# Half of the low parts of the weights in the key-head stage, on GpSimd instead of VectorE

## The chip, the cores and the metric

The kernel runs on one core of a Trainium2 chip. The metric is the device time of one execution in microseconds, as the median of several runs; before the change it was 2585.1 us. The engines go by the names of the profile: PE is TensorE, DVE is VectorE, ACT is ScalarE, POOL is GpSimd, and SP issues most of the transfers. Each engine works through its own list of instructions in order and waits at an instruction until what it needs is there.

## What is computed

The reference is a two-layer trunk over 256 latent tokens and 256 context tokens of 2048 features, all in float32. Layer 1 is attention. Layer 2, which the text calls the delta layer, is a bidirectional gated DeltaNet; it projects the normalized tokens, runs a short convolution and solves a small triangular system in each chunk of 64 tokens:

```python
qkv, z, b_raw, a_raw = split_cols(h, DN_SPLITS)          # h @ w_in: 16 key heads, 32 value heads of 128
qkv = jax.nn.silu(depthwise_conv(qkv, conv_w))
...
kb = kf * bf[..., None]
lmat = jnp.where(strict, jnp.einsum('bhncd,bhnsd->bhncs', kb, kf) * decay, 0.0)
rhs = jnp.concatenate([vf * bf[..., None], kb * jnp.exp(gf)[..., None]], axis=-1)
sol = lax.linalg.triangular_solve(lmat + jnp.eye(CHUNK, dtype=F32), rhs, left_side=True, lower=True)
```

A scan over the chunks, a norm, a gate and an output projection follow.

## The kernel before

**Matrix products in two parts.** Activations and weights are each split into a high part in a rounded float32 form (float32r) and a low part, the remainder. A product is three matmuls for every block of 128 contraction rows: high x high, high weight x low activation, low weight x high activation. These are lines 90, 91 and 92 in `dense`; the tiles are `whi`, `wlo` for the weights and `hh`, `hl` for the activations. All three follow one another on PE for each block, so the low part of a weight tile is needed at almost the same moment as the high part.

**A unit of the projection.** `dunit` makes 128 outputs of the delta layer's input projection. `load_split` loads the unit's 128 x 2048 weights in two tiles of 128 x 1024 (`load_raw`, SP's queue, line 71; four `raw` buffers in rotation), and `split` makes of each tile the high part on ACT (line 77) and the low part on DVE (line 78): raw minus high, three buffers each for `whi` and `wlo`. A `raw` buffer is free again when its low part is made. 16 blocks of contraction, and so 48 matmuls, follow on PE. `dunit` is called for 67 units: one for strengths and decays (`U_BA`), 16 for the keys over all 512 tokens, 16 for the queries and 32 for the gates over 256 tokens, and two for the values of head 0. Later value units do not pass through it: in the scans, `hi` and `lo` do the same splitting at lines 1080 and 1088 from a list `W`, in an order of PE, DVE and ACT that is written out by hand.

**The key-head stage.** From about 1120 to 1764 us the kernel goes through the 16 key heads. `head` (a generator, cut into steps by `yield`) projects keys and queries, convolves them (`conv_taps`, line 561, DVE), transposes the keys (line 679, PE), makes the decays (line 711 on POOL, the product at line 713 on PE, the exponential at line 716 on ACT) and the systems of two directions (lines 731 to 737, DVE). `inverse` inverts the 32 x 32 blocks of two heads at a time: transposes into `L` (line 755, DVE), 31 steps of an outer product (line 768) and a subtraction (line 770) on DVE, a scaling on POOL (line 772), transposes (lines 775, 776, DVE), then products of blocks on PE (lines 786 and 798). `zunits` projects the gates. These three are woven by hand: six steps of `heads`, then for each further step of `heads` seven steps of `inverse`, with the gates' units dealt out between them.

POOL has little else in this stage: memsets (lines 751, 752, 762, 763), the two small operations on the key norms (lines 701 and 702), line 711 and line 772.

**What sets the order.** Outside the scans, the order of each engine's instructions is made by the framework's planner when the kernel is built, from the program's order and its own estimate of each instruction's time. It also inserts the semaphores. A change of the engine of one instruction can so change the order of others.

Of the kernel before, what the change touches and what calls it, by code (L numbers as in the profile page):

```python
# [26 lines left out]
def trunk_kernel(ctx: ExitStack, tc: tile.TileContext, g):  # L27
# [40 lines left out]
    # ---------------------------------------------------------------- helpers  # L68
# [5 lines left out]
    def split(raw, m=1024):  # L74
        hi = wp.tile([128, 1024], F32R, name="whi", tag="whi", bufs=3)
        lo = wp.tile([128, 1024], F32R, name="wlo", tag="wlo", bufs=3)
        A.copy(hi[:, :m], raw[:, :m])  # L77
        V.tensor_tensor(lo[:, :m], raw[:, :m], hi[:, :m].bitcast(F32), op=ALU.subtract)  # L78
        return hi, lo

    def load_split(src, n=2048):
        return [split(load_raw(src[:, c:min(n, c + 1024)], min(1024, n - c)), min(1024, n - c))
                for c in range(0, n, 1024)]
# [11 lines left out]
    def sliced(wsrc, units, k0, n, xh, xl, pst, first, last):  # L95
        # n contraction tiles of two units
        m = 128 * n
        raw = wp.tile([128, 1024], F32, name="raw", tag="raw", bufs=4)
        for e in range(2):
            nc.sync.dma_start(raw[:, m * e:m * e + m], wsrc[units[e]][:, 128 * k0:128 * k0 + m])  # L100
        w = split(raw, 2 * m)
        for e in range(2):
            dense(pst[e], [w], m * e, n, xh, xl, k0=k0, first=first, last=last)
# [3 lines left out]
    def adaln(l, ps, pm, tp, order, bufs=3, after=None):  # L107
        # a step for every two weight tiles
        wm, bmod, gain = ((g["ab_wm"], ab_bmod, ab_gain), (g["dn_wm"], dn_bmod, dn_gain))[l]
        for f0, n in order:  # L110
            # n blocks of 128 outputs from f0 on
# [35 lines left out]
    def adaln_lanes(l, ps, pm, tp, chunks, after=None):  # L147
        # the sums over the contraction tiles on the vector engine, those over the partitions at the end
# [36 lines left out]
    def rstd_bcast(squares, nb, dim, ps, tag, tp, sq_tag="sq"):  # L185
        # squares: for every block of tokens the tiles that add up to its squares, summed over the feature tiles
        ss = ps.tile([128, 4], F32, name="ss", tag=tag, bufs=1)
        for tb in range(nb):
            for i, t in enumerate(squares[tb]):
                PE.matmul(ss[:, tb:tb + 1], t, ones[:, 0:1], start=i == 0, stop=i == len(squares[tb]) - 1)  # L190
        ms = tp.tile([128, 4], F32, name="ms", tag="ms")
        V.tensor_scalar(ms[:, :nb], ss[:, :nb], 1.0 / dim, EPS, op0=ALU.mult, op1=ALU.add)  # L192
        rs = tp.tile([128, 4], F32, name="rs", tag="rs")
        P.tensor_tensor(rs[:, :nb], ms[:, :nb], half[:, :nb], op=ALU.pow)  # L194
        dg = tp.tile([128, 4, 128], F32, name="dg", tag=sq_tag)
        rb = ps.tile([128, 512], F32, name="rb", tag=tag, bufs=1)
        for tb in range(nb):
            V.tensor_scalar(dg[:, tb], ident, rs[:, tb:tb + 1], None, op0=ALU.mult)
            PE.matmul(rb[:, tb * 128:(tb + 1) * 128], ones, dg[:, tb], start=True, stop=True)
        return rb  # L200
# [4 lines left out]
    def add_squares(acc, srcs, first, tp, n=T, sq_tag="sq", last=False):  # L205
        # the last squares stay apart
# [29 lines left out]
    # ================================================================ layer 0  # L236
# [6 lines left out]
    with tc.tile_pool(name="s0", bufs=2) as tp, tc.tile_pool(name="s0p", bufs=1, space=PSUM) as ps:  # L243
# [6 lines left out]
        # squares, four feature tiles at a time  # L250
# [51 lines left out]
    with tc.tile_pool(name="ab", bufs=2, reuse_waits="tile") as tp, \  # L302
# [29 lines left out]
        def parts(src, name, n=T, scale=1.0, pool=None, bufs=1):  # L332
            # float32 as the sum of two float32r
# [16 lines left out]
        def attend(qT, kT, vT, h, bias=None, rope=None):  # L350
            # v to token-major
# [58 lines left out]
        # latent ranks and the shared rope key  # L410
# [98 lines left out]
    # ================================================================ layer 1  # L509
    # Tokens of a sequence go in two tiles of two chunks, (0, 3) and (1, 2); inside a tile the order is  # L510
    # (half of the chunk, chunk of the pair, token), so that a 32-partition quadrant is 2 * half + chunk,
    # while the keys are worked on, and (chunk of the pair, token) in the scans.
# [23 lines left out]
    def dunit(u, sl):  # L536
        w = load_split(DW[u])
# [29 lines left out]
    def tile_act(dst, src, func, halves):  # L567
        # to tile order, as (half, chunk, token) or (chunk, token)
# [9 lines left out]
    def by_pair(dst, src):  # L578
        # columns from (half, chunk, token) to (chunk, half, token)
        A.copy(dst.rearrange("p s (h b i) -> p s b h i", h=2, b=2), src.rearrange("p s (b h i) -> p s b h i", b=2, h=2))  # L580

    def by_chunk(dst, src):
        # rows from (half, chunk, token) to (chunk, token)
# [22 lines left out]
    def project(u, p):  # L606
        # output unit to the residual, back from tile order
# [5 lines left out]
    # the scans take over the room of the keys' tiles tag by tag, so that they begin as it is left  # L613
    with tc.tile_pool(name="dn", bufs=2, reuse_waits="tile") as tp, \
            tc.tile_pool(name="dnps", bufs=2, space=PSUM, reuse_waits="tile") as ps:
        # write strength and decay of all heads
# [3 lines left out]
        # of the keys: squared norms inverted, and norms, as the rows lie here and in the scans; of the queries, what  # L620
        # stands for the norm's epsilon once they are not normalized
# [35 lines left out]
        for d in range(2):  # L657
# [3 lines left out]
            # scan arrangement a: chunk h of a pair runs in direction (a + h) % 2  # L661
# [10 lines left out]
        def head(kh):  # L672
# [31 lines left out]
            # the decays [row, column]: forwards for the transposed system, backwards for the system  # L704
            # itself and, within the sequence, transposed
# [27 lines left out]
            for d in range(2):  # L733
                # of a 32-block only what lies on its side of the diagonal is read
# [8 lines left out]
        def inverse(sg):  # L743
            # (norm^2 / beta + L)^-1 of two heads, their keys not normalized, L the system forwards and its transpose backwards: of the
            # 32-blocks on the vector engine, with the unit on the partition
            NTu = NTs[sg].rearrange("p a k s h i -> p (a k s h) i")
            # as the blocks come and transposed
# [31 lines left out]
            # the block between the two halves of a chunk  # L779
# [42 lines left out]
        def mix(main, filler, n):  # L822
            # one step of the filler after every n of the main work
# [8 lines left out]
        def woven():  # L832
            # the heads one after the other, each with its products begun while the one before it ends
# [71 lines left out]
        def cut(t, i, shape):  # L905
            # piece i of a tile, in a shape
# [11 lines left out]
        # block-diagonal operands: the zeros stay, the blocks come from memory  # L918
# [14 lines left out]
        # of keys and values, the parts that the state's products take  # L933
# [6 lines left out]
        def blocks(dst, src):  # L940
            # [128, 2 (direction), 4, 64] in memory to [128, 2 (arrangement), 4, 128]
# [25 lines left out]
        def step(o, n):  # L967
            # one chunk in both directions, in four parts
# [68 lines left out]
        def finish(o):  # L1037
            # norm and gate of a head, in four parts
# [26 lines left out]
        # of the output products, units below NE take the heads below 12 early  # L1065
        NE = 8
        # weight tiles in the order of their use
# [23 lines left out]
        def tile_mm(p, j, k0, xh, xl, sl, first, last):  # L1091
            # the eight contraction tiles of weight tile j, one at a time
# [12 lines left out]
        def value_unit(q):  # L1105
            # q: unit number after those of head 0; its first step is 2 * q - 2
# [57 lines left out]
        for st in range(-2, 64 + LAG):  # L1164
# [27 lines left out]
            # what follows the products of the unit before  # L1192
# [77 lines left out]
def _layout(inputs):  # L1270
# [5 lines left out]
    def fm(a):  # [tok, feat] -> [128, feat/128, tok]  # L1276
        return np.ascontiguousarray(a.T.reshape(-1, 128, a.shape[0]).transpose(1, 0, 2))

    def units(w, kt=None):  # [K, C] -> [C/128, 128, K/128 * 128]
# [3 lines left out]
    def vec(v):  # [F] -> [128, F/128]  # L1283
# [25 lines left out]
    # neighbourhood bias, padded outside the window  # L1309
# [10 lines left out]
    # constants of the shapes alone  # L1320
# [10 lines left out]
    # gated delta layer  # L1331
# [45 lines left out]
```

## Time and profile before

| | |
|---|---|
| median of 3 runs | 2585.1 us (2583.42 to 2586.82) |
| span of the profiled execution | 2580.0 us |
| PE busy in it | 2499.2 us (97%) |
| DVE busy | 1852.2 us (72%) |
| ACT busy | 1146.6 us (44%) |
| POOL busy | 267.4 us (10%) |
| the key-head stage | about 1120 to 1764 us |

The span is the time from the first to the last instruction of one execution. Rows of groups read: line, engine, operation, output tile <- input tiles, shapes, count | busy us, mean ns of one | idle us of the engine just before them and what ended it. Rows of waits read: who waited <- for whom: us in total, times, the longest. A timeline row is start, length, engine, line, operation, and in brackets how long the engine had been idle and what ended that. Busy figures of PE are higher than its true use, as consecutive matmuls overlap in the record.

### The profile page before, as it was taken

The numbers are of one execution on the slowest core, as the hardware profiler recorded it, in microseconds if no ns is written. First come the engines' busy times: TensorE is split into PE (matmuls) and PEld (weight loads), VectorE is DVE, ScalarE is ACT, GpSimd is POOL, SyncE is SP. The second block draws the span as 40 slices with busy tenths as digits, with TensorE's granted clock in tenths as the row PEclk, the third lists the DMA queues.
The fourth block names the chain that finished last, engine by engine and source line by source line (L and its number), as shares of the span: only waits on it lengthen the run. The fifth ranks groups of instructions, "written<-read, shape, count | busy, mean of one in ns | idle before, by whom it ended". The sixth has DMA issues, their size and how long they took to land.

```text
span 2580.0 us, 43446 instructions
## 1 busy us (share of the span) xinstructions
PE 2499.2 (97%) x16586; PEld 2039.0 (79%) x16586; DVE 1852.2 (72%) x3543; ACT 1146.6 (44%) x2484; POOL 267.4 (10%) x261
## 2 busy tenths in 40 slices
PE   6999999999999999989999999999999999999998
PEld 4657888888767788768888889897777777777898
DVE  4544788773455687758999999987677777777754
ACT  4223323232333422377656655643444445445353
POOL 0000000000000000133212222310000000003000
PEclk9999999999999999999999999999999999999999
DMA  8872655532343376644454544563333433335454
GB/s 258 289 247 90 201 172 167 175 114 96 117 153 100 120 230 221 212 139 157 142 156 152 160 138 150 159 213 100 88 99 115 119 99 106 113 91 174 153 188 140
DMA packets 201810, 394.30 MB, mean 153 GB/s; under 512 B 68225, under 2 KB 109697, under 8 KB 201473
## 3 DMA queue, kind: packets, MB, share of 16 engines
q1 hardware_dynamic: 200448, 389.98, 47.9%
q8 instruction: 131, 2.15, 0.4%
q10 hardware_dynamic: 1152, 1.54, 0.2%
q14 instruction: 79, 0.64, 0.1%
HBM read 356.28 MB, written 35.13 MB: 152 GB/s over the span
## 4 chain that ended last, share of the span: by engine, by line
PE 79%; DVE 9%; issue 6%; DMA 3%; ACT 2%; SPq 0%; POOL 0%; DVEq 0%; POOLq 0%; ACTq 0%
PE mm L90 19%; PE mm L91 18%; PE mm L92 18%; PE pks L982 3%; PE pmod L127 3%; DVE wlo L78 2%; PE sp L348 2%; PE ptr L994 2%; DVE X L770 1%; DVE outer L768 1%; PE po L348 1%; PE pu L798 1%; DVE acc L561 1%; PE ptr L1027 1%; PE psu L1013 1%
## 5 line engine op out<-in xcount | busy, mean ns | idle before, releaser
L90 PE MATMUL mm<-hh,whi 128*128 128x512 f32 (+1 forms) x2784 | 988.5, 355 | 3.7 <-ACT t L636 2.2
L92 PE MATMUL mm<-hh,wlo 128*128 128x512 f32 (+1 forms) x2784 | 962.2, 346 | 8.7 <-DVE wlo L78 7.5
L91 PE MATMUL mm<-hl,whi 128*128 128x512 f32 (+1 forms) x2784 | 963.2, 346 | 0.0
L77 ACT CAST whi<-raw 128x1024 fp32r<-128x1024 f32 (+2 forms) x346 | 338.3, 979 | 668.4 <-PE mm L91 515.6
L90 PEld LDWEIGHTS mm<-hh,whi 128*128 128x128 f32 x2784 | 535.7, 192 | 113.8 <-issue 32.6
L92 PEld LDWEIGHTS mm<-hh,wlo 128*128 128x128 f32 x2784 | 535.4, 192 | 73.1 <-DVE wlo L78 9.4
L91 PEld LDWEIGHTS mm<-hl,whi 128*128 128x128 f32 x2784 | 536.0, 193 | 62.2 <-issue 8.4
L78 DVE TENSOR_TENSOR wlo<-raw,whi 128x1024 fp32r<-128x1024 f32 (+2 forms) x346 | 402.7, 1166 | 212.9 <-ACT whi L77 206.1
L163 DVE SCALAR_TENSOR_TENSOR lacc<-mraw,cond,lacc 128x512 f32<-128x512 f32 x300 | 208.8, 749 | 0.0
L561 DVE SCALAR_TENSOR_TENSOR acc<-cin,taps,acc 128x508 f32<-128x508 f32 (+3 forms) x256 | 196.1, 767 | 6.7 <-ACT acc L552 4.3
L1004 DVE SCALAR_TENSOR_TENSOR vl<-ptr,egm,vh 128x128 fp32r<-128x128 f32 x224 | 64.6, 346 | 98.3 <-ACT rf L1001 39.4
L711 POOL TENSOR_TENSOR rhs<-ghl,incl 128x512 fp32r<-128x512 f32 (+1 forms) x96 | 108.4, 1139 | 133.4 <-PE pd L713 114.2
L127 PE MATMUL pmod<-mraw,cond 128*32 128x512 f32 (+2 forms) x640 | 94.3, 501 | 23.2 <-DMA mraw<-ab_wm 18.6
L768 DVE SCALAR_TENSOR_TENSOR outer<-L,bv,X 128x31 f32<-128x31 f32 (+15 forms) x248 | 112.4, 453 | 4.7
L1088 DVE TENSOR_TENSOR wlo<-raw,whi 128x1024 fp32r<-128x1024 f32 x84 | 102.6, 1222 | 14.4 <-ACT whi L1080 13.8
L194 POOL TENSOR_TENSOR rs<-ms,half 128x4 f32<-128x4 f32 (+1 forms) x5 | 4.7, 947 | 985.1 <-DVE ms L192 985.1
L770 DVE TENSOR_TENSOR X<-X,outer 128x31 f32<-128x31 f32 (+15 forms) x248 | 101.7, 410 | 4.6
L575 ACT ACTIVATE ac<-acc 128x128 f32<-128x128 f32 x160 | 37.4, 300 | 146.0 <-DVE acc L561 146.0
L90 PE MATMUL mm<-gh,whi 128*128 128x512 f32 x256 | 99.9, 392 | 1.7 <-DVE x1B L493 1.7
L91 PE MATMUL mm<-gl,whi 128*128 128x512 f32 x256 | 99.9, 390 | 0.2 <-DVE gl L481 0.2
L92 PE MATMUL mm<-gh,wlo 128*128 128x512 f32 x256 | 99.7, 390 | 0.0
L998 ACT ACTIVATE vh<-ptr,egm 128x128 fp32r<-128x128 f32 x224 | 71.0, 373 | 56.6 <-PE ptr L994 54.6
(289 smaller groups left out, 3629.2 us busy)
## 6 DMA issues: line engine op xcount, KB each, us to landing
raw<-dn_w SPq DMA_DIRECT2D x194, 512.0 KB, 4.0
mraw<-dn_wm SPq DMA_DIRECT2D x96, 512.0 KB, 4.7
mraw<-ab_wm SPq DMA_DIRECT2D x88, 512.0 KB, 5.4
raw<-ab_w SPq DMA_DIRECT2D x66, 512.0 KB, 3.8
raw<-dn_wo SPq DMA_DIRECT2D x64, 512.0 KB, 3.7
raw<-ab_wo SPq DMA_DIRECT2D x32, 512.0 KB, 4.6
raw<-ab_w SPq DMA_DIRECT2D x32, 256.0 KB, 3.6
spt<-sp SPq DMA_DIRECT2D x64, 128.0 KB, 2.8
```

Source lines behind the costliest of these rows:

```text
L77: A.copy(hi[:, :m], raw[:, :m])
L78: V.tensor_tensor(lo[:, :m], raw[:, :m], hi[:, :m].bitcast(F32), op=ALU.subtract)
L90: PE.matmul(ps, wh[:, c], xh[:, k0 + k, sl], start=first and k == 0, stop=False)
L91: PE.matmul(ps, wh[:, c], xl[:, k0 + k, sl], start=False, stop=False)
L92: end = PE.matmul(ps, wl[:, c], xh[:, k0 + k, sl], start=False, stop=last and k == kt - 1)
L127: PE.matmul(pmod[32 * q:32 * q + 32, :m], cond[:, 4 * kg + q, :], raw[c // 1024][:, half + c % 1024:half + c % 1024 + m], start=kg == 0, s ...
L163: V.scalar_tensor_tensor(acc[:, s], raw[:, q], cond[:, k, s:s + 1], acc[:, s], op0=ALU.mult, op1=ALU.add)
L561: V.scalar_tensor_tensor(o3[:, :, i0:i1], p3[:, :, i0 + d:i1 + d], taps[:, ch, t:t + 1], o3[:, :, i0:i1], op0=ALU.mult, op1=ALU.add)
L711: P.tensor_tensor(rhs, ghl[i].bitcast(F32)[:, d, kh * 8:kh * 8 + 2 * n].unsqueeze(2).broadcast_to(sh), incl[:, c].unsqueeze(1).broadcast_t ...
L768: V.scalar_tensor_tensor(o, L[:, rows, k:k + 1].broadcast_to([128, n, m]), bv[:, k:k + 1], X[:, k:k + 1, cols].broadcast_to([128, n, m]), ...
L770: V.tensor_tensor(X[:, rows, cols], X[:, rows, cols], o, op=ALU.subtract)
L1088: V.tensor_tensor(w, raws[j], h.bitcast(F32), op=ALU.subtract)
```

## The change

`split` takes an engine for the subtraction, VectorE unless another is given. `load_split` takes a tuple of engines and deals them to its tiles in turn. `dunit` passes VectorE and GpSimd, so that in each of its units the low part of the first tile is made on VectorE and that of the second on GpSimd. Every other caller goes on as before. Apart from this the diff removes comments only.

```diff
-    def split(raw, m=1024):
+    def split(raw, m=1024, by=None):
         hi = wp.tile([128, 1024], F32R, name="whi", tag="whi", bufs=3)
         lo = wp.tile([128, 1024], F32R, name="wlo", tag="wlo", bufs=3)
         A.copy(hi[:, :m], raw[:, :m])
-        V.tensor_tensor(lo[:, :m], raw[:, :m], hi[:, :m].bitcast(F32), op=ALU.subtract)
+        (by or V).tensor_tensor(lo[:, :m], raw[:, :m], hi[:, :m].bitcast(F32), op=ALU.subtract)
         return hi, lo
 
-    def load_split(src, n=2048):
-        return [split(load_raw(src[:, c:min(n, c + 1024)], min(1024, n - c)), min(1024, n - c))
+    def load_split(src, n=2048, by=(None,)):
+        return [split(load_raw(src[:, c:min(n, c + 1024)], min(1024, n - c)), min(1024, n - c), by[c // 1024 % len(by)])
                 for c in range(0, n, 1024)]
...
     def dunit(u, sl):
-        w = load_split(DW[u])
+        w = load_split(DW[u], by=(V, P))
```

## Prediction

> **What bounds the kernel now.** I first counted what moves (the page's list of DMA issues), then cut the trace into stretches and kept those that hold the key-head stage (1120 to 1764 us).
>
> ```profile
> raw<-dn_w SPq DMA_DIRECT2D x194, 512.0 KB, 4.0
> ...
> 1120.00:1190.00 70.00, 64.81 (x401) 55.69 (x400) 45.47 (x71) 55.85 (x121) 22.59 (x20) 0.94 0.37 116
> 1190.00:1690.00 500.00, 477.66 (x4668) 436.64 (x4667) 469.08 (x775) 309.66 (x595) 131.91 (x139) 0.97 0.50 156
> 1690.00:1764.00 74.00, 71.28 (x643) 64.66 (x642) 64.63 (x114) 27.86 (x51) 5.92 (x7) 0.98 0.54 165
> ```
>
> The columns after the length are the busy us of PE, PEld, DVE, ACT and POOL, then clock, DMA share and GB/s. In the 500 us from 1190 on, which I call the window, PE is busy 478, DVE 469 and POOL 132: the matmuls and VectorE share the bound, with 31 us of idle DVE, and GpSimd has room. The third stretch is the quiet one, because POOL hardly works there. Of the 194 weight loads, 60 belong to the value units of the scans (30 units of two tiles, list `W`), so `dunit` has 134 tiles, and 67 of them move.
>
> Does DVE set the pace or only fill its time? The chain of work that ended last, followed within 1120 to 1750 us, says both engines do; the waits of PE in the window and the wait of SP within the stage say where they meet:
>
> ```profile
> by line: PE mm L92 12.7%; PE mm L90 12.6%; PE mm L91 12.5%; DVE wlo L78 9.1%; DVE X L770 5.4%; DVE outer L768 5.3%; issue 5.1%; PE pu L798 4.6%; DVE acc L561 4.1%; DMA raw<-dn_w 3.2%; PE px L786 3.2%; DVE U L776 2.7%; PE pd L713 1.4%; PE kk
> ...
> PE ptk L679 <- ACT ac L572: 14.0, 6, 3.7
> PE mm L92 <- DVE wlo L78: 5.1, 7, 1.6
> ...
> SPq L71 <- DVE wlo L78: 187.8, 51, 7.6
> ```
>
> About 45% of that chain is matmuls of the rows named and 27% is DVE (9.1 + 5.4 + 5.3 + 4.1 + 2.7). The reader is to see that PE seldom waits for a low part itself (5.1 us, 7 times); it waits longer for the convolution's results (14.0 us), which DVE made late, and the next raw load waits for a low part to be done with its buffer.
>
> **The change, part by part: what leaves DVE.** The groups of DVE in the window, and the same groups in the quiet stretch:
>
> ```profile
> L78 DVE TENSOR_TENSOR wlo<-raw,whi 128x1024 fp32r<-128x1024 f32 x103 | 131.4, 1276 | 13.3 <-ACT whi L77 8.4 <-PE pd L713 3.8 <-DMA raw<-dn_w 0.7
> L768 DVE SCALAR_TENSOR_TENSOR outer<-L,bv,X 128x255 f32<-128x255 f32 (+15 forms) x204 | 95.4, 468 | 3.7
> L770 DVE TENSOR_TENSOR X<-X,outer 128x255 f32<-128x255 f32 (+15 forms) x204 | 87.2, 428 | 3.4
> L561 DVE SCALAR_TENSOR_TENSOR acc<-cin,taps,acc 128x510 f32<-128x510 f32 (+3 forms) x104 | 72.8, 700 | 0.0
> ...
> L737 DVE TENSOR_TENSOR sp<-DT,QKm 128x256 f32<-128x256 f32 x14 | 10.6, 754 | 0.0
> ...
> L737 DVE TENSOR_TENSOR sp<-DTo,QKm 128x256 f32<-128x256 f32 x14 | 5.9, 420 | 1.9 <-ACT DTo L716 1.9
> ```
>
> ```profile
> L768 DVE SCALAR_TENSOR_TENSOR outer<-L,bv,X 128x231 f32<-128x231 f32 (+15 forms) x41 | 16.2, 396 | 1.0
> L78 DVE TENSOR_TENSOR wlo<-raw,whi 128x1024 fp32r<-128x1024 f32 x13 | 15.7, 1220 | 6.2 <-ACT whi L77 6.1
> L770 DVE TENSOR_TENSOR X<-X,outer 128x240 f32<-128x240 f32 (+15 forms) x42 | 14.2, 339 | 1.1
> ```
>
> Half of the 103 low parts, 51.5, move: 51.5 x 1.276 = 65.7 us leave DVE in the window. Were that all, DVE would fall to 403 of 500 us and the change would gain.
>
> **What it costs on GpSimd.** The trace has no such subtraction of a weight tile on POOL, but the same operation on the same shape runs at L1129, and the multiplication of L772 is of the same length:
>
> ```profile
> 2322.24 2.36 POOL L1129 TENSOR_TENSOR hl<-re,hh 128x1024 fp32r<-128x1024 f32 x1 [6.77 <-ACT hh L1128]
> 2324.55 2.83 POOL L1129 TENSOR_TENSOR hl<-gin,hh 128x1024 fp32r<-128x1024 f32 x1
> ...
> L772 POOL TENSOR_TENSOR X<-X,bv 128x1024 f32<-128x1024 f32 x6 | 11.5, 1918 | 44.9 <-DVE X L770 44.9
> ...
> L711 POOL TENSOR_TENSOR rhs<-ghl,incl 128x512 fp32r<-128x512 f32 (+1 forms) x82 | 90.2, 1109 | 100.2 <-PE pd L713 100.1
> ```
>
> I take 2.4 us, by the first L1129, the undisturbed one of the same operation; the ends are 1.92 (L772) and 2.83. POOL's own load in the window grows from 132 by 51.5 x 2.4 = 124 to 256 of 500 us, which it can carry. [...]
>
> **What the two engines take from each other.** This is the term that decides. What DVE and POOL did at 1223.7 us and at 1250.7 us:
>
> ```profile
> 1223.26 0.42 DVE L770 TENSOR_TENSOR X<-X,outer 128x247 f32<-128x247 f32 x1
> 1223.71 1.34 DVE L768 SCALAR_TENSOR_TENSOR outer<-L,bv,X 128x240 f32<-128x240 f32 x1
> ...
> 1225.09 1.13 DVE L770 TENSOR_TENSOR X<-X,outer 128x240 f32<-128x240 f32 x1
> ...
> 1223.74 2.21 POOL L711 TENSOR_TENSOR rhs<-ghl,incl 128x512 fp32r<-128x512 f32 x2 [14.93 <-PE pd L713]
> ...
> 1250.72 4.13 DVE L755 STREAM_TRANSPOSE L<-NT 64x1024 f32<-64x1024 f32 x2
> ...
> 1250.89 1.92 POOL L772 TENSOR_TENSOR X<-X,bv 128x1024 f32<-128x1024 f32 x1 [8.16 <-DVE X L770]
> ```
>
> L768 averages 0.40 us in the quiet stretch; with two POOL operations beginning at the same moment it took 1.34, and the L770 behind it 1.13 where its neighbour of about that size took 0.42. The two transposes, which read one operand, ran beside a POOL operation of 1.92 us in 4.13, twice their usual 2.05 (the row of L755 below). So a DVE operation that reads two SBUF operands stands still while POOL reads, and one with a single operand doesn't. [...]
>
> ```profile
> L776 DVE STREAM_TRANSPOSE U<-X 64x1024 f32<-64x1024 f32 x12 | 26.4, 2201 | 0.0
> L755 DVE STREAM_TRANSPOSE L<-NT 64x1024 f32<-64x1024 f32 x12 | 24.5, 2045 | 0.1
> L775 DVE STREAM_TRANSPOSE U<-X 64x1024 f32<-64x1024 f32 x12 | 23.6, 1967 | 0.2
> ```
>
> How much is lost per us of POOL? Against the quiet stretch, DVE's groups in the window are longer by: L768 204 x (468 - 396) = 14.7 us, L770 204 x (428 - 339) = 18.2, L78 103 x (1276 - 1220) = 5.8, L737 14 x (754 - 420) = 4.7, together 43 us, and some of L561, whose shapes the quiet stretch doesn't all have. POOL's L711 were busy 90.2 us. That is at least 0.48 us of DVE lost per us of POOL. From above: the two-operand groups (131.4 + 95.4 + 87.2 + 72.8 + 10.6 + 5.9 = 403) fill 0.81 of the 500 us, so no more than 0.81 can be lost. Part of L711's 90.2 is its own waiting for DVE, as the second of the pair above shows, so the loss per us of reading lies above 0.48: I take 0.7, towards the upper end.
>
> **The sum.** One moved tile gives DVE 1.28 us and takes 2.4 x 0.7 = 1.68, a loss of 0.40 us. In the window that is 51.5 x 0.40 = +21 us of DVE, 469 to 490. Ends: 51.5 x (1.92 x 0.48 - 1.28) = -18 us and 51.5 x (2.83 x 0.81 - 1.28) = +52 us. How much of +21 reaches the time? Nothing, if all of the 31 us of idle DVE could be filled; all of it and a little more (21/0.94 = 22), if DVE goes on being busy 94% of the time. Both have ground: PE's matmuls hold the other half of the chain, but much of the idle is DVE waiting for a cast (8.4 us before L78). I take the middle and a bit, 14 us. The stage has some 126 low parts against the window's 103, so 14 x 126/103 = 17, and 1 us for the two low parts outside and for GpSimd's small operations of each head, which DVE already waits for and which now queue behind 2.4 us tiles:
>
> ```profile
> DVE km L703 <- POOL nrm L701: 5.3, 6, 1.6
> ```
>
> The casts on ScalarE, the loads and all matmuls stay as many as they are, and after 1764 us nothing of the change runs. The profiled execution spans 2580.0 us and the median of the runs is 2585.1, so 5.1 us lie around the span or between executions. 2580 + 18 = 2598 for the span, **2603 us** as a time.
>
> The planner sets every engine's order anew from these costs as it believes them. I cost that at nothing for the mean and give it 10 us either way in the ranges.
>
> **The rivals.**
>
> *Faster: the lock costs less than the tile gives.* It decides at a loss share of 1.28/2.4 = 0.53, between my bounds of 0.48 and 0.81. For it: POOL may begin its tiles while DVE is transposing (L755, L775 and L776 take 26.4 + 24.5 + 23.6 = 74.5 us of the window) or idle, and PE's wait for low parts (5.1 us) and part of the 14.0 for the convolution could go. Against: 0.48 counts POOL's own waiting as reading. At its end, 18 us less DVE in the window, 22 in the stage, a bit over half of it gained: about 2573. [...]
>
> *No change: PE carries the stage.* If the idle 31 us of DVE takes the +21, the matmuls set the end as before: 2580 to 2590.
>
> *Much slower: tiles stuck on GpSimd.* POOL runs its instructions in order, and it stands waiting for most of the window:
>
> ```profile
> POOL nrm L701 <- ACT junk L682: 120.6, 13, 13.1
> POOL rhs L711 <- PE pd L713: 100.1, 53, 14.9
> POOL X L762 <- DVE U L776: 64.0, 6, 11.6
> ```
>
> A weight tile that the planner puts behind one of these comes late, PE stops at its third matmul (each contraction tile needs the low part at once), and so does the load that wants its raw buffer. Two tiles of prefetch cover a few us. If one of three moved tiles (21 of 63) were late by 1.9 us, the mean wait of L711 (100.1/53), it would add 40 to my 18: 2643. Against it: those waits are of a POOL with nothing else to do, and a tile that is ready sooner is planned ahead of them.
>
> *The change does less than it says* is out: each `dunit` passes the pair, tile 0 goes to V and tile 1 to P.
>
> **How the numbers follow.** Forecast (2590 to 2630) 0.50; stuck tiles (over 2630) 0.13; no change (2580 to 2590) 0.18; faster (below 2580) 0.19. About 0.2%, 5 us, is what a measurement of this kernel can tell from no change. Slower by more than that is 0.50 + 0.13, rounded to 0.63; same 0.18; faster 0.19. The range takes in the faster case's 2573 and the stuck tiles' 2643: 2572 to 2643, with about 0.1 left out on each side. The likeliest case's own range is 2590 to 2630.
>
> **What would show it.** In the new profile: POOL has 67 new groups `wlo<-raw,whi` of 2.4 us or more (1.9 would speak for the faster rival); L78 on DVE halves in count; L768, L770 and L561 grow by what the lock takes, L770 from 428 to some 500 ns; DVE's busy time over the stage rises or stays although 63 tiles left. If L770 and L768 stay as they are, the lock term is wrong and the time falls. If PE shows long waits for a low part from POOL, the stuck tiles are right. If DVE's busy time rises and the stage is no longer, PE was the bound alone.

## The result and the profile after

| | before | after |
|---|---|---|
| median of 4 runs each, side by side | 2584.57 us (2583.42 to 2586.82) | 2650.43 us (2648.64 to 2653.76) |
| ratio, 95% interval | | 1.0261 [1.0246, 1.0276] |
| span of the profiled execution | 2580.0 us | 2652.0 us |

The change makes the kernel 2.6% slower. 2603 us had been forecast, with a range up to 2643: the sign was right, the size was not. Four rows of the page after, the span, the granted clock in 40 slices, the groups of low parts on DVE and on POOL:

```profile
span 2652.0 us, 43434 instructions
...
PEclk9999999999999999988988998999999999999999
...
L78 DVE TENSOR_TENSOR wlo<-raw,whi 128x1024 fp32r<-128x1024 f32 (+2 forms) x279 | 321.1, 1152 | 216.5 <-ACT whi L77 213.0
L78 POOL TENSOR_TENSOR wlo<-raw,whi 128x1024 fp32r<-128x1024 f32 x67 | 172.3, 2571 | 593.4 <-ACT whi L77 577.2
```

The 67 tiles are there, at 2.57 us each. The clock's row shows 8s in the stage (slices of 66 us); in the page before it is 9 in all 40.

To compare the same work, the stage is measured from 1120 us to its last block products (line 798, within 3 us): 1790 before, 1859 after. Stretches, with columns as in the prediction (length, then busy us of PE, PEld, DVE, ACT and POOL, clock, DMA share, GB/s), before and after:

```profile
1120.00:1790.00 670.00, 638.42 (x6025) 577.22 (x6024) 594.48 (x974) 403.95 (x791) 163.00 (x169) 0.96 0.49 150
```

```profile
1120.00:1859.00 739.00, 670.61 (x6005) 599.78 (x6005) 606.17 (x911) 412.26 (x791) 327.60 (x236) 0.91 0.45 136
```

The stage is 69 of the 72 us by which the profiled execution is longer. DVE's own work grew by only 606.17 - 594.48 = 12 us. PE's busy time grew by 32 us for the same matmuls, and its idle time (length less busy) from 31.6 to 68.4, by 37. So the question is where PE waits, and why its matmuls take longer. The groups of DVE in these stretches, before and after:

```profile
L78 DVE TENSOR_TENSOR wlo<-raw,whi 128x1024 fp32r<-128x1024 f32 x127 | 163.2, 1287 | 28.4 <-ACT whi L77 23.4 <-PE pd L713 3.8 <-DMA raw<-dn_w 0.7
L768 DVE SCALAR_TENSOR_TENSOR outer<-L,bv,X 128x31 f32<-128x31 f32 (+15 forms) x248 | 112.4, 453 | 4.7
L770 DVE TENSOR_TENSOR X<-X,outer 128x31 f32<-128x31 f32 (+15 forms) x248 | 101.7, 410 | 4.6
L561 DVE SCALAR_TENSOR_TENSOR acc<-cin,taps,acc 128x510 f32<-128x510 f32 (+3 forms) x140 | 99.0, 709 | 1.1 <-ACT acc L552 0.8
```

```profile
L768 DVE SCALAR_TENSOR_TENSOR outer<-L,bv,X 128x31 f32<-128x31 f32 (+15 forms) x248 | 142.9, 576 | 6.4
L561 DVE SCALAR_TENSOR_TENSOR acc<-cin,taps,acc 128x510 f32<-128x510 f32 (+3 forms) x140 | 131.6, 942 | 18.4 <-ACT acc L552 17.3
L770 DVE TENSOR_TENSOR X<-X,outer 128x31 f32<-128x31 f32 (+15 forms) x248 | 118.4, 478 | 6.2
L78 DVE TENSOR_TENSOR wlo<-raw,whi 128x1024 fp32r<-128x1024 f32 x63 | 83.5, 1326 | 32.3 <-ACT whi L77 30.0 <-DMA raw<-dn_w 1.3 <-PE mm L92 0.9
```

64 low parts left (80 us of L78), and three groups whose work did not change grew by 30.5, 32.6 and 16.7 us, together 80: the relief is paid back in full, and smaller groups bring the 12 us more. What PE waits for, before and after (total us, times, longest):

```profile
PE ptk L679 <- ACT ac L572: 15.2, 7, 3.7
PE mm L92 <- DVE wlo L78: 7.5, 8, 2.4
```

```profile
PE ptk L679 <- ACT ac L572: 29.3, 14, 5.3
PE mm L92 <- DVE wlo L78: 24.3, 8, 4.0
PE pd L713 <- POOL rhs L711: 4.9, 2, 4.1
```

PE never waits for a low part from POOL here. It waits for DVE most of all: for the convolution, which ScalarE passes on (line 572), and for low parts that DVE makes. A third wait, absent before, is for the masks that line 711 makes on POOL.

**One wait, followed through.** The timeline after, a few rows of POOL, DVE, ACT and PE from 1296 to 1307 us (start, length, engine, line):

```profile
1296.79 2.66 POOL L78 TENSOR_TENSOR wlo<-raw,whi 128x1024 fp32r<-128x1024 f32 x1
1297.11 2.61 DVE L768 SCALAR_TENSOR_TENSOR outer<-L,bv,X 128x256 f32<-128x256 f32 x1
...
1299.40 2.25 POOL L711 TENSOR_TENSOR rhs<-ghl,incl 128x256 fp32r<-128x256 f32 x2
...
1299.65 1.09 DVE L561 SCALAR_TENSOR_TENSOR acc<-cin,taps,acc 128x510 f32<-128x510 f32 x1
...
1303.69 0.74 DVE L561 SCALAR_TENSOR_TENSOR acc<-cin,taps,acc 128x508 f32<-128x508 f32 x1
...
1304.51 1.28 ACT L572 ACT_TABLE_LOAD   x1 [4.43 <-DVE acc L561]
...
1304.80 0.48 DVE L768 SCALAR_TENSOR_TENSOR outer<-L,bv,X 128x252 f32<-128x252 f32 x1
...
1305.80 0.91 ACT L572 ACTIVATE ac<-acc 128x128 f32<-128x128 f32 x4
...
1306.16 0.33 PE L679 MATMUL ptk<-ident,ac 128*128 128x128 f32 x1 [3.33 <-ACT ac L572]
```

POOL's subtraction holds an L768 for 2.61 us that takes 0.48 undisturbed. The convolution behind it ends late, ACT had stood 4.43 us waiting for it, and PE stands 3.33 us. The same moments as stretches:

```profile
1302.00:1303.00 1.00, 0.83 (x8) 0.63 (x6) 1.00 (x2) 0.00 (x0) 0.67 (x1) 1.00 0.37 148
1303.00:1306.00 3.00, 0.00 (x0) 0.00 (x0) 2.96 (x5) 1.48 (x2) 0.49 (x1) 1.00 0.00 0
1306.00:1307.00 1.00, 0.84 (x7) 0.84 (x8) 1.00 (x4) 0.98 (x5) 0.00 (x0) 0.93 0.00 0
1307.00:1310.00 3.00, 3.00 (x16) 3.00 (x15) 3.00 (x8) 2.96 (x7) 0.58 (x1) 0.50 0.51 175
1310.00:1311.00 1.00, 1.00 (x9) 1.00 (x9) 1.00 (x1) 0.75 (x5) 1.00 (x1) 0.87 0.49 111
```

After the idle 3 us, the clock is 0.50 for over 3 us: 16 pieces of matmul work fill 3 us where 8 filled 0.83 of one. **This wait of PE was paid a second time, as slow matmuls behind it.** Some 3.4 us at half clock follow an idle stretch of 3.33 us; the clock fell only some 0.7 us after PE had begun again (1306.16 and about 1306.9). Over the whole stage the slower clock is all of PE's added busy time: busy time times granted clock is 638.42 x 0.96 = 613 us before and 670.61 x 0.91 = 610 after.

### The profile page after: what moved, and what is told of

Read it like the earlier page. It is cut to its first block, busy times and chain, and to the rows that moved or that the text cites. A ratio compares the mean times of both kernels' runs of the same rounds, so it can differ in the third digit from the quotient of the medians.

```text
span 2652.0 us, 43434 instructions
## 1 busy us (share of the span) xinstructions
PE 2535.1 (96%) x16586; PEld 2062.0 (78%) x16586; DVE 1862.6 (70%) x3476; ACT 1155.4 (44%) x2490; POOL 440.1 (17%) x328
## 4 chain that ended last, share of the span: by engine, by line
PE 74%; DVE 14%; issue 5%; DMA 3%; ACT 2%; POOL 1%; SPq 0%; DVEq 0%; POOLq 0%; ACTq 0%
PE mm L90 18%; PE mm L92 17%; PE mm L91 17%; PE pks L982 3%; DVE acc L561 3%; PE pmod L127 3%; DVE X L770 2%; DVE outer L768 2%; PE sp L348 2%; PE ptr L994 2%; DVE wlo L78 2%; PE po L348 1%; DVE U L776 1%; PE pu L798 1%; PE ptr L1027 1%
## 5 line engine op out<-in xcount | busy, mean ns | idle before, releaser
L90 PE MATMUL mm<-hh,whi 128*128 128x512 f32 (+1 forms) x2784 | 999.0, 359 | 2.8 <-ACT t L636 2.2
L92 PE MATMUL mm<-hh,wlo 128*128 128x512 f32 (+1 forms) x2784 | 973.8, 350 | 25.4 <-DVE wlo L78 24.3
L90 PEld LDWEIGHTS mm<-hh,whi 128*128 128x128 f32 x2784 | 544.7, 196 | 113.2 <-issue 31.1
L92 PEld LDWEIGHTS mm<-hh,wlo 128*128 128x128 f32 x2784 | 544.1, 195 | 93.6 <-DVE wlo L78 26.8
L78 DVE TENSOR_TENSOR wlo<-raw,whi 128x1024 fp32r<-128x1024 f32 (+2 forms) x279 | 321.1, 1152 | 216.5 <-ACT whi L77 213.0
L78 POOL TENSOR_TENSOR wlo<-raw,whi 128x1024 fp32r<-128x1024 f32 x67 | 172.3, 2571 | 593.4 <-ACT whi L77 577.2
L561 DVE SCALAR_TENSOR_TENSOR acc<-cin,taps,acc 128x508 f32<-128x508 f32 (+3 forms) x256 | 228.6, 894 | 23.1 <-ACT acc L552 20.0
L768 DVE SCALAR_TENSOR_TENSOR outer<-L,bv,X 128x31 f32<-128x31 f32 (+15 forms) x248 | 142.9, 576 | 6.4
L770 DVE TENSOR_TENSOR X<-X,outer 128x31 f32<-128x31 f32 (+15 forms) x248 | 118.4, 478 | 6.2
L92 PE MATMUL mm<-gh,wlo 128*128 128x512 f32 x256 | 99.7, 389 | 0.0
```

Of the source, the lines that this page charges most:

```text
L78: (by or V).tensor_tensor(lo[:, :m], raw[:, :m], hi[:, :m].bitcast(F32), op=ALU.subtract)
L90: PE.matmul(ps, wh[:, c], xh[:, k0 + k, sl], start=first and k == 0, stop=False)
L92: end = PE.matmul(ps, wl[:, c], xh[:, k0 + k, sl], start=False, stop=last and k == kt - 1)
L561: V.scalar_tensor_tensor(o3[:, :, i0:i1], p3[:, :, i0 + d:i1 + d], taps[:, ch, t:t + 1], o3[:, :, i0:i1], op0=ALU.mult, op1=ALU.add)
L768: V.scalar_tensor_tensor(o, L[:, rows, k:k + 1].broadcast_to([128, n, m]), bv[:, k:k + 1], X[:, k:k + 1, cols].broadcast_to([128, n, m]), ...
L770: V.tensor_tensor(X[:, rows, cols], X[:, rows, cols], o, op=ALU.subtract)
```

## The experiments

In the expectations A is: the new order of the engines costs most; B: the lock between DVE and POOL alone (DVE's two-operand work held up while POOL reads, as the L768 of 2.61 us above); C: tiles stuck on POOL. The theories A1, A2, A3 and W are versions of A, told where they come up. Unless said, a kernel was timed against the kernel before beside it (medians 2580.7 to 2582.8 us).

To hold an order, the program is traced twice in the build: one variant is planned and its order read, then the other is planned with an edge of order, without a semaphore of its own, from each instruction to the next on its engine.

```diff
+    def build(low, order=None):
...
+            if order is not None:
...
+                for engine, places in order.items():
+                    last = None
+                    for n in places:
...
+                        if last is not None:
+                            tc.add_manual_dep(traced[n], last, info, reason="order")
+                        last = traced[n].name
```

`build(work, order)` stands for it below, with the second low part of each unit made on POOL ("P") or on DVE ("V"). The order is that of PE, DVE, ACT and SP; POOL's is free.

**Order, relief and lock taken apart (e1 to e3).** e1 is the change's work in the order of before, e2 the work of before in the order of the change, e3 the relief without POOL's reading: POOL subtracts 8 columns and fills the other 1016 columns of the second tile with two memsets, so these columns of the low part are left out. A memset waits only for a free buffer, so in e3 POOL can also do part of a tile's work ahead of the cast, and the `raw` buffer comes free sooner.

```diff
+    return build("P", order of "V")
+    return build("V", order of "P")
+    return build("R", order of "V")
...
+            P.tensor_tensor(lo[:, :8], raw[:, :8], hi[:, :8].bitcast(F32), op=ALU.subtract)
+            for _ in range(2):
+                extra.append(P.memset(lo[:, 8:m].bitcast(F32), 0.0).ins.name)
```

> The changed kernel, but PE, DVE, ACT and SP go through their instructions in the order that the kernel before has; only the 67 moved low parts are taken out of DVE's list and run on POOL, where the planner places them. Theory A (the new order costs the most: the planner, which knows nothing of the lock, rearranged the engines, and DVE now stands at instructions whose inputs are late): the lock alone stays, DVE busy in the stage again some 20 us above before, time 2595 to 2612. Theory B (lock and the slower low part cost it, in any order): 2635 to 2655. Theory C (low parts come late from POOL's list): 2630 or more, and PE waits for a low part of POOL for tens of us.

> All low parts on DVE, as before, but PE, DVE, ACT and SP in the order that the changed kernel has; the planner places the 67 low parts in DVE's list. Theory A: most of the loss is there without any GpSimd work, 2620 to 2645. Theory B and theory C: within 10 us of before, 2575 to 2595.

> The order of before on PE, DVE, ACT and SP. The moved low parts are left out of the computation but for 8 columns, which POOL subtracts; it fills the other 1016 columns with zeros, twice over, so that it takes about 2.2 us a tile and reads next to nothing. DVE is relieved, and little is locked. If the lock is what eats the relief: DVE busy in the stage falls by 65 to 80 us, L770 and L768 stay at the means of before, and the time is 2555 to 2580. If the relief is worth nothing at all because PE sets the pace: 2580 to 2590. Theory C (late low parts): as slow as with the subtraction, 2600 or more.

Measured: e1 2616.77 us, ratio 1.0132 [1.0111, 1.0154]; e2 2632.72, 1.0184 [1.0151, 1.0216]; e3 2547.36, 0.9861 [0.9837, 0.9886]. The stage of e1, of e2 and of e3, each to its last block products:

```profile
1120.00:1825.00 705.00, 652.24 (x5993) 588.25 (x5994) 617.85 (x910) 404.38 (x791) 320.18 (x235) 0.94 0.47 143
```

```profile
1120.00:1838.00 718.00, 658.30 (x5994) 590.37 (x5995) 589.63 (x977) 413.60 (x793) 164.16 (x169) 0.93 0.46 140
```

```profile
1120.00:1755.00 635.00, 621.97 (x5987) 563.18 (x5988) 521.81 (x913) 407.19 (x793) 296.89 (x363) 0.98 0.52 159
```

| against before | time | DVE busy | PE idle | PE busy |
|---|---|---|---|---|
| e3, relief, old order | -35 us | -73 | -19 | -16 |
| e1, relief, lock and queue, old order | +34 | +23 | +21 | +14 |
| e2, new order alone | +50 | -5 | +28 | +20 |
| the change | +66 | +12 | +37 | +32 |

The relief is worth 35 us, what POOL's subtractions bring with them (e1 less e3) costs 69, and the order of the change another 34 (2650 against 2617). Taken the other way round, the new order costs 50 and GpSimd's work in that order only 18 (2650 against 2633), so the parts do not simply add. A and B both hold a part, and neither alone the whole. In every row PE's busy time follows its idle time, 0.65 to 0.9 us for one: the clock, both ways, as busy time times clock is 610 to 613 us in all five stages.

The 69 us are not the lock alone. Between e3 and e1, DVE's busy time grows by 96 us, but the largest of PE's waits in e1 is for POOL, and that for the convolution is shorter than before (15.2 us):

```profile
PE pd L713 <- POOL rhs L711: 16.8, 8, 4.2
PE mm L92 <- DVE wlo L78: 13.2, 6, 4.1
PE ptk L679 <- ACT ac L572: 8.3, 8, 2.2
```

One of the eight, on POOL and then on PE:

```profile
1399.84 3.04 POOL L78 TENSOR_TENSOR wlo<-raw,whi 128x1024 fp32r<-128x1024 f32 x1 [5.29 <-ACT whi L77]
1402.84 3.82 POOL L711 TENSOR_TENSOR rhs<-ghl,incl 128x256 fp32r<-128x256 f32 x3
...
1404.49 0.58 PE L713 MATMUL pd<-rhs,seg 128*128 128x256 f32 x1 [3.83 <-POOL rhs L711]
```

POOL had waited for the cast of a moved tile, then made its low part, and the masks stood behind it in POOL's list. Such a queue needs no lock. No run separates the two in time. In the change the planner's order keeps this wait to 4.9 us.

POOL was about as busy in e3 as in e1 (297 and 320 us); with memsets, which read nothing, DVE kept its pace. Its groups, a memset beside a convolution in the timeline, and the group of memsets on POOL:

```profile
L773 DVE SCALAR_TENSOR_TENSOR outer<-L,bv,X 128x31 f32<-128x31 f32 (+15 forms) x248 | 111.1, 448 | 9.1 <-POOL X L768 4.0
L775 DVE TENSOR_TENSOR X<-X,outer 128x31 f32<-128x31 f32 (+15 forms) x248 | 99.8, 402 | 5.1
```

```profile
1334.12 0.74 DVE L566 SCALAR_TENSOR_TENSOR acc<-cin,taps,acc 128x510 f32<-128x510 f32 x1
...
1334.21 0.94 POOL L81 MEMSET wlo<- 128x1016 f32 x1
...
1334.78 0.35 DVE L773 SCALAR_TENSOR_TENSOR outer<-L,bv,X 128x135 f32<-128x135 f32 x1
```

```profile
L81 POOL MEMSET wlo<- 128x1016 f32 x128 | 121.3, 947 | 92.7 <-PE mm L97 87.8 <-DMA raw<-dn_w 4.1
```

(L773, L775 and L566 there are 768, 770 and 561 elsewhere.) 448 and 402 ns are the values of before, against 576 and 478 in the change. C falls for the tiles themselves: PE waits for no low part from POOL in e1 either. What came late from POOL's list in e1 were the masks.

**Which belief of the planner makes the bad order (e4 to e8, e11).** The runs rest on the assumption that the planner estimates each instruction by itself, and so sees less work on DVE (the relief) and not the lock. All but e7 and e8 have the work of before and only the order of another plan: a second low part planned 960 wide (e4, plan "W"), 64 wide (e5, "N"), made twice (e6, "T"), and narrow and twice in turn, so that the sum is right (e11, "M"). e7 and e8 have the change's work, in plans that believe in a second low part made twice ("T"), or with 256 columns made twice ("B"). These plan letters are not those of the theories. A1 says that a plan costs what it wrongly believes of DVE, A2 that any new plan scatters, A3 that the sum of DVE's work must be right.

```diff
+        if odd and low == "N":
+            V.tensor_tensor(lo[:, :64], raw[:, :64], hi[:, :64].bitcast(F32), op=ALU.subtract)
+        elif odd and low == "T":
+            V.tensor_tensor(lo[:, :m], raw[:, :m], hi[:, :m].bitcast(F32), op=ALU.subtract)
+            extra.append(V.tensor_tensor(lo[:, :m], raw[:, :m], hi[:, :m].bitcast(F32), op=ALU.subtract).ins.name)
...
+    return build("V", order of "W")
+    return build("V", order of "N")
+    return build("V", order of "T")
+    return build("P", order of "T")
+    return build("P", order of "B")
+    return build("V", order of "M")
```

> The work of before, all low parts on DVE. The order of PE, DVE, ACT and SP is that which the planner makes for a kernel whose second low part of each unit is 960 columns wide instead of 1024: a plan that is new, but believes DVE to be as loaded as it is to within 0.07 us a tile. Theory A1 (a plan costs what its false belief costs): within 10 us of before, 2573 to 2593. Theory A2 (any new plan scatters by tens of us, and the plan of before is a lucky one): 2600 to 2640.

> The work of before, in the order planned for a kernel whose second low part of each unit is 64 columns wide, on DVE: the planner believes DVE to be relieved by some 1.1 us a tile and knows nothing of GpSimd. Theory A1: as slow as the order of the changed kernel with all low parts on DVE (2633), 2615 to 2645. If it was GpSimd's queue in the plan and not DVE's relief that spoiled the order: 2575 to 2595. Theory A2 gives no number other than that of the run before this one.

> The work of before, in the order planned for a kernel that makes every second low part twice on DVE: the planner believes DVE to be busier by 1.2 us a tile than it is. Theory A1, a false belief on the other side: DVE takes its work later than it could, but nothing stands waiting at its head; 2570 to 2600. Theory A2: 2600 to 2640, like any new plan.

> The changed kernel, second low parts on GpSimd, in the order planned as in the run before this one. With the lock, DVE loses some 23 us net, so this plan is nearer to the truth than that of before. Theory A1: at or below the 2617 of the same work in the order of before, 2590 to 2620. Theory A2: 2620 to 2660.

> The changed kernel, second low parts on GpSimd, in the order planned for a kernel that makes them all on DVE and then does 256 columns of each second one again: the planner believes every moved tile to cost DVE some 0.4 us more, which is about what the lock takes net (+23 us over 63 tiles in the run with the order of before). Theory A1 (a plan costs what it believes wrongly): no slower than the 2617 in the order of before, 2590 to 2617, and what then stays over 2582 is the lock's own. Against A1: 2625 or more.

> The work of before, in the order planned for a kernel in which the second low part is 64 columns wide in every other unit and made twice in the units between: the planner is wrong by 1.1 us a tile on each, but right on the sum. Theory A3 (what spoils an order is a wrong sum of DVE's work, by which the planner weaves the systems' inversion, the convolutions and the products together at another pace): within 10 us of before, 2573 to 2595. Theory A2 (every plan other than that of before loses): 2600 to 2630.

| | median us | ratio, 95% |
|---|---|---|
| e4, 960 wide | 2586.02 | 1.0004 [0.9992, 1.0016] |
| e5, 64 wide | 2623.52 | 1.0162 [1.0145, 1.018] |
| e6, twice | 2649.62 | 1.0258 [1.0242, 1.0273] |
| e7, GpSimd, twice | 2675.37 | 1.0353 [1.0324, 1.0383] |
| e8, GpSimd, 256 columns twice | 2636.14 | 1.0215 [1.0197, 1.0232] |
| e11, narrow and twice in turn | 2598.61 | 1.007 [1.0047, 1.0094] |

A nearly right plan costs nothing, a plan with too little DVE work 41 us, and one with too much 67. e6 missed the expectations from A1 and from A2, and e7 and e8, which should have helped the change by believing in more DVE work, did not bring it to 2617; e7 is slower than either theory allowed. e11, with the sum right, comes nearest after e4; at 2598.6 us, with single runs from 2588.5 to 2611.2, it lies between what A3 and A2 asked and settles neither. In these runs a plan made for another amount of DVE work is bad in either direction; paying the lock into the sum is no cure.

**The weave of the inversion (e13, e14).** W says that the loss sits in how lines 561, 768 and 770 alternate on DVE. Only these were held to the order of before: in e13 on the narrow plan with the work of before, in e14 on the change's own plan and work.

```diff
+                    for n in places:
+                        if only and traced[n].name not in WEAVE:
+                            continue
...
+    return build("V", order of "N", first held to the weave of "V")
+    return build("P", order of "V", weave only)
```

> The work of before and the false belief of the narrow plan (second low parts 64 columns wide, 2624 us), but the planner is bound to one thing of the order of before: how the steps of the inversion (L768, L770) follow the convolutions' (L561) in DVE's list. All else of DVE, PE, ACT and SP it plans by its false belief. Theory W (the new order loses because the inversion runs ahead of the heads' convolutions, by 4 of them on the mean): 2580 to 2600. If other parts of the false plan cost it: 2615 to 2630.

> The changed kernel, second low parts on GpSimd and planned so, bound to that same weave of before in DVE's list and free in all else. Theory W: the order's share of the loss goes and the lock's stays, 2605 to 2630, about the 2617 of the run with the whole order of before. If other parts of the plan cost it: 2640 to 2655.

Measured: e13 2609.0 us, 1.0109 [1.0091, 1.0127]; e14 2647.86, 1.026 [1.0243, 1.0277]. Some 14 of e5's 41 us come back, so that e13 falls between its two ranges, and next to nothing of the change's. W holds a third of e5's loss and is not the cause of the change's.

**The lock that was there before (e9, e10, e12).** POOL's line 711 reads too. It was moved to DVE (e9) and to ACT (e10, as 640 small operations), with plans of their own, and to ACT in the order of before (e12).

```diff
-                    P.tensor_tensor(rhs, ghl[i].bitcast(F32)[:, d, kh * 8:kh * 8 + 2 * n].unsqueeze(2).broadcast_to(sh),
+                    V.tensor_tensor(rhs, ghl[i].bitcast(F32)[:, d, kh * 8:kh * 8 + 2 * n].unsqueeze(2).broadcast_to(sh),
...
+                    for u in range(2 * n):
+                        A.activation(rhs[:, u], incl[:, c], AF.Copy, scale=ghl[i].bitcast(F32)[:, d, kh * 8 + u:kh * 8 + u + 1])
```

> The kernel before, with the masks of the decays (L711, 96 operations) made on DVE instead of GpSimd, planned anew. DVE takes on some 57 us of work (64 of 0.69 and 32 of 0.42) and loses the 48 us or more that GpSimd's reads took from it; the plan now knows what DVE does. If the lock charges DVE as much as the trace of before suggests: DVE busy about as before, time within 15 us of before, 2567 to 2597. If the lock charged little: DVE some 50 us busier, 2610 or more.

> The kernel before, with the masks of the decays made on ACT in 640 small operations of some 0.2 us, planned anew. DVE loses the lock of L711 and takes on nothing: L768 and L770 fall to the means of the quiet stretch (0.40 and 0.34 us), DVE busy falls by 40 us or more. If ACT bears the 130 us more: 2550 to 2575, a kernel that beats both. If ACT, busy 61% of the stage already, becomes late with the casts: 2590 or more.

> The kernel before in its own order, with the masks of the decays (L711) made on ACT in 640 small operations, which the planner puts between ACT's other work; POOL reads next to nothing in the stage. The lock takes 48 us or more from DVE before: if DVE's relief is worth here what it was worth in the run without the lock (35 us for 73 us of DVE), 2555 to 2570. If ACT's 130 us more make the casts late: 2590 or more; then the run with a plan of its own lost to ACT and not to its order.

Measured: e9 2617.04 us, 1.0139 [1.0118, 1.016]; e10 2607.21, 1.0091 [1.0059, 1.0122]; e12 2656.85, 1.0294 [1.0277, 1.0312]. All are slower, by 26 to 75 us. On DVE the lock's price shows all the same: in e9 the masks put 56.0 us on DVE, and its busy time in the stage is still 590 us (594 before), as the first expectation said, while the time missed its range; in e10, where they went to ACT, DVE's busy time is 542, and ACT bore 164 us of them instead of the 130 expected. e12's groups of DVE (lines 768, 561 and 770 are 783, 572 and 785 there):

```profile
L89 DVE TENSOR_TENSOR wlo<-raw,whi 128x1024 fp32r<-128x1024 f32 x127 | 154.9, 1221 | 105.1 <-ACT whi L77 99.7 <-PE pd L728 4.8
L783 DVE SCALAR_TENSOR_TENSOR outer<-L,bv,X 128x31 f32<-128x31 f32 (+15 forms) x248 | 99.0, 399 | 4.7
L572 DVE SCALAR_TENSOR_TENSOR acc<-cin,taps,acc 128x510 f32<-128x510 f32 (+3 forms) x138 | 85.6, 622 | 2.6 <-ACT acc L563 2.2
L785 DVE TENSOR_TENSOR X<-X,outer 128x31 f32<-128x31 f32 (+15 forms) x248 | 84.4, 340 | 4.6
```

Against the rows of before: 248 x (453 - 399) + 248 x (410 - 340) + 138 x (709 - 622) + 127 x (1287 - 1221) = 51 us of DVE that line 711 cost. They did not become time in e12, where ACT was now late: low parts on DVE waited 99.7 us for casts.

**One engine's order at a time (e15 to e18).** DVE alone in the order of the change, or PE alone, with the work of before and everything else planned anew around it; then DVE alone or PE alone in the order of before, with the change's work. D: DVE's order carries the cost; E: PE's does; S: any order but the one of before costs.

```diff
+    return build("V", order of DVE of "P")
+    return build("V", order of PE of "P")
+    return build("P", order of DVE of "V")
+    return build("P", order of PE of "V")
```

> All low parts on VectorE as before. DVE alone is held to the order it has after the change; PE, ACT and SP are planned anew around it. Theory D (the new order costs by the order in which DVE takes its work): near the 2633 of the all-new order, 2622 to 2645, with DVE waits inside the stage (casts, queries' sums) as large as there. Theory E (it costs by PE's order of matmuls): PE is free here, so 2582 to 2605. Theory S (any order other than the one before costs, whichever engine has it): 2600 to 2620, and the four runs of this set lie close together, each pair within 15.

> All low parts on VectorE as before. PE alone is held to the order it has after the change; DVE, ACT and SP are planned anew around it. Theory D: DVE is free, so 2582 to 2605. Theory E: near the 2633 of the all-new order, 2622 to 2645. Theory S: 2600 to 2620.

> The change's work, every second low part on GpSimd. DVE alone is held to the order from before; PE, ACT and SP are planned anew around it. Theory D: the order's 34 us come back, 2608 to 2626, as with all engines in the old order (2617). Theory E: PE is free to be as bad as in the change, 2640 to 2660. Theory S: 2630 to 2650.

> The change's work, every second low part on GpSimd. PE alone is held to the order from before; DVE, ACT and SP are planned anew around it. Theory D: DVE's order is the planner's again and the order's cost stays, 2640 to 2660. Theory E: 2608 to 2626. Theory S: 2630 to 2650.

Measured: e15 2635.74 us, 1.0212 [1.0195, 1.0228]; e16 2644.17, 1.0245 [1.0228, 1.0261]; e17 2637.71, 1.0217 [1.0195, 1.0239]; e18 2640.73, 1.0229 [1.0213, 1.0244]. With either engine's new order held and the rest planned around it, all that the whole new order lost (2633) is lost, and either old order alone gives back only 10 to 13 of the 34 us. D is right for e15 and e18 and wrong for e16 and e17; E is right for e16 alone and wrong for e15 and e18; S has e17, e18 and the closeness of the four, but puts e15 and e16 16 us or more too low. What the four share is that PE and DVE no longer stand in the pairing of before; that this is the cause is not shown. The waits of PE in e2, in e16 and in e18 differ in kind:

```profile
PE ptk L679 <- ACT ac L572: 31.6, 14, 5.8
PE mm L92 <- DVE wlo L78: 15.2, 8, 5.5
```

```profile
PE px L786 <- DVE U L776: 31.0, 3, 14.0
PE ptk L679 <- ACT ac L572: 19.0, 11, 5.4
```

```profile
PE pd L713 <- POOL rhs L711: 27.1, 14, 4.7
```

e2 loses at the convolution and at low parts, e16 at the results of the inversion, and e18, which has PE's old order and the tiles on POOL like e1, at the masks. **What stays open** is which property of the order of before keeps these waits short; it is no single wait and no single engine's order.

No version here that does all the work is faster than the kernel before.

## Why the prediction was right in sign and wrong in size

- **What moves, and POOL's price: right.** 67 tiles; 2.4 us was taken, the median on the chip is 2.41 and the mean 2.57.
- **The lock: right, and near in size.** 1.68 us of DVE per tile was taken. (One reading on the way to it was not what it said: the 420 ns for line 737 stand in the window itself and not in the quiet stretch. The term holds all the same, as the slow one of the two takes 418 ns in e12.) e1 less e3 gives 617.85 - 521.81 = 96 us over 64 tiles, 1.5 each, more than the 1.28 that a tile frees and less than the 2.4 x 0.81 = 1.9 of the upper bound: 0.59 us lost per us of POOL (1.5/2.56), between the bounds 0.48 and 0.81 and above the 0.53 at which the faster rival would begin. DVE's net of 21 us in the window comes to 21 x 126/103 = +26 us in the stage; e1 shows +23, the change +12. Of e1's +23 the tiles' lock less their relief is 64 x (1.5 - 1.28) = 14; the other 9 are in e3 too, where the low parts left on DVE run beside line 711 more often than before and take 1.42 us on average; those beside a memset alone take 1.21, much as those beside nothing (1.22). The rival "the lock costs less than the tile gives" is out, and with it the gain.
- **From DVE to time: mis-sized.** The step took 14 of 21 us, with all of it "and a little more" as the upper end. In the order of before, +23 us of DVE went with +34 us: about +21 of PE idle and +14 of PE busy. Two things were missing. First, the idle did not come through the convolution there: PE waited 16.8 us for masks that stood behind moved tiles on POOL (none before) and 5.7 us more for low parts of DVE. The sum had 1 us in all for work that queues behind the tiles, and named the small operations on the norms, not the masks. Second, it had no term for the clock (0.96 before, 0.94 in e1), which makes the +14. e3 shows the same in the other sign: -19 of idle came with -16 of busy. That the half clock makes the second part rests on the traces (busy time times clock stays the same) and was not tested by a run of its own. The idle time of DVE was read as slack that it could fill; yet in e3 less work on DVE took 19 us off PE's idle time, so PE had been waiting for DVE all the same.
- **The new order: the step that failed.** "I cost that at nothing for the mean and give it 10 us either way." It cost 34 us in the change (2650 against 2617 in the old order) and 50 alone (e2). In the old order the change stays within the forecast's range; the new order takes it out. That the planner counted the relief and not the lock is a likely reason, not a shown one. e6 and e8 show that a plan with more DVE work is no better, and e15 to e18 that neither PE's nor DVE's order alone is to blame.
- **Rivals.** "PE carries the stage" is out: the stage follows DVE in both directions (e1, e3). "Tiles stuck on GpSimd" gave the nearest time, 2643, which was luck: its mechanism did not happen. PE never waited for a low part from POOL in the change, and POOL stood 156 us waiting for casts (row below). Nearest to it comes e1, where not the tiles but the masks behind them were late:

```profile
L78 POOL TENSOR_TENSOR wlo<-raw,whi 128x1024 fp32r<-128x1024 f32 x64 | 163.7, 2558 | 172.4 <-ACT whi L77 156.2 <-DMA spk<-sp 10.3 <-DMA spt<-sp 3.6
```

- **What would show it.** L78 on DVE did halve, L768 and L561 did grow, L770 in the stage to 478 where some 500 was said, and DVE's busy time did not fall although 64 tiles left it.

From kernel to kernel the steps are: relief -35, POOL's subtractions with their lock and their queue +69, order +34. They end at the change by construction, so that their sum of +68 (+66 against the kernel before beside it) does not test them; by the other path the order is +50 and GpSimd's work +18.

## What to carry to other kernels

Before work goes from VectorE to GpSimd, set the time that VectorE is freed (1.28 us here) against what GpSimd's reading takes from two-operand VectorE work (1.5 us here, e1 less e3), not against GpSimd's idle time, and look at what would stand behind the moved work in GpSimd's list. Where the planner decides the order, a changed cost is a new order: cost it from runs, by timing the same work in the other plan, and hold the old order to see the change itself. Where the matmuls nearly fill the span, as here (95% of the stage before), count the waits of TensorE nearly twice: each us added to its idle time came here with 0.65 to 0.9 us more of busy time, at a lower granted clock.

## What the runs showed of the hardware that was not expected

- One us of PE idle went with 0.65 to 0.9 us more PE busy time, in four kernels and in both directions, while busy time times granted clock stayed at 610 to 613 us; the stage's mean granted clock ran from 0.98 (e3) to 0.91 (the change) with its idle time from 13 to 68 us.
- GpSimd's memsets left VectorE alone: with 121 us more of them, L768 took 448 ns against 453 before, while 164 us of subtractions (the change) made it 576. VectorE's transposes, which read one operand, kept their means in the stage: 1.97 to 2.19 us before, 1.98 to 2.19 in the change.
- Line 711 had already cost VectorE about 51 us before the change, 0.47 us for each us that it is busy on GpSimd, by its row of before in the stage:

```profile
L711 POOL TENSOR_TENSOR rhs<-ghl,incl 128x512 fp32r<-128x512 f32 (+1 forms) x96 | 108.4, 1139 | 133.4 <-PE pd L713 114.2 <-ACT ghl L655 17.0 <-DVE ghl L656 1.9
```
